# The order of the products inside an MLP layer's first matrix product: eight mixed orders, or three sweeps

## The chip, the cores and the metric

The kernel runs on one core of one Trainium2 chip. The metric is the time of one execution on the device in microseconds (us), taken as the median of several runs. Five engines work side by side, each on its own queue of instructions: TensorE (PE; its weight loads are shown as PEld), VectorE (DVE), ScalarE (ACT), GpSimd (POOL) and SyncE (SP), which here issues the transfers. PSUM is where matmuls add up their sums, SBUF where everything else lies.

## The reference

Two layers of a decoder trunk over 256 tokens of width 2048, each followed by an MLP of width 8192. All weights and all data are float32.

```python
def _mlp(h, w1, w2):
    u = jnp.einsum('bsd,df->bsf', h, w1)
    u = jnp.square(jax.nn.relu(u))
    return jnp.einsum('bsf,fd->bsd', u, w2)
...
    for i in range(DEPTH):
        h = _rmsnorm(x, mix_norm[i])
        j = i // N_MIXERS
        if i % N_MIXERS == 0:
            x = x + _rglru_block(h, ...)
        else:
            x = x + _dilated_attention_block(h, ...)
        x = x + _mlp(_rmsnorm(x, mlp_norm[i]), mlp_w1[i], mlp_w2[i])
    return _rmsnorm(x, final_norm)
```

## The kernel before

**Products in three parts.** Each float32 number is cut into a high part (its rounding to the type that TensorE multiplies, fp32r) and a low part (the rest, rounded too). A product is the sum of three: high weights by high data, high weights by low data, low weights by high data. The low by low product is left out.

**Units.** All weights come as units of 128 x 2048 numbers (1 MB) in the order in which they are used. For each unit SP issues a load into a `raw` buffer (3 of them, line 76), ScalarE copies it to the high tile `whi` (4 buffers, line 86), and VectorE subtracts to get the low tile `wlo` (3 buffers, line 90). `before_unit` (line 103) issues these ahead of the unit's products: loads 5 units ahead, high parts 3, low parts 2. The items of the program run in a fixed order; `after(n, ...)` puts a piece of follow-up work behind the item n places later. Every engine takes its instructions in the order in which they are issued.

**The data.** `xT` holds the layer's input, transposed: for each of 16 steps k (128 of the 2048 input features) a row of 512 columns, columns 0 to 255 the high part of the 256 tokens, columns 256 to 511 their low part. The four tiles `xT0` to `xT3` hold four steps each; `transpose_chunk` (lines 169 to 183) makes them, with TensorE transposes (line 176), ScalarE for the high part (line 158) and VectorE for the low part (line 159).

**The first MLP product** (`plan_mlp`, from line 504). The 8192 hidden features are worked on in four stretches of 16 units; a unit gives 128 hidden features for all 256 tokens. Its weights stand still in TensorE (128 x 128 a matmul), and the rows of `xT` move through. For each of the 16 steps there are the pieces ("h", k, 0, 256), ("h", k, 256, 512) and ("l", k, 0, 256): which weight tile, which step, which columns of `xT`; "h" with 0 to 512 is the first two in one matmul of 512 columns. `orders` (line 225) lists the pieces of a unit in one of seven styles, and each of the eight stretches (four in either MLP) has a style of its own. In the order of time: thirds, wide_first, pairs, apart in the first MLP, thirds_low_first, fours, thirds, as_was in the second. `stand_w2` (line 252) issues them through `mm` (line 141, one weight load and one matmul each) into a PSUM bank `acc` (four of them). In the two styles that begin with "thirds", all three pieces go into the same 256 columns of the bank; in the others the product with the tokens' low part has columns 256 to 511 for itself. In the first stretch of either MLP the first two units are done on steps 0 to 11 first, then on 12 to 15, since the last tile of `xT` is still being made.

**What follows a unit.** `u_done` (line 488): where there are two half sums, VectorE adds them (a reduction, line 493) and then takes the maximum with 0 and multiplies by the norm's factor (line 494); where there is one, a single instruction does the latter out of PSUM (line 491). ScalarE squares (line 496) and makes the high part `aT` (line 498); VectorE makes its low part one item later (line 502).

**The second MLP product** follows each stretch (`out_item`, line 281, and `stand_x`, line 265). There `aT` stands still and the weights move, 512 columns a matmul: high by high, high by low, low by high. It takes 16 units too. The recurrent layer's first projection uses `stand_w` (line 216) with the order high, high, low of "thirds".

Of the kernel before, what the change touches and what calls it, by code (L numbers as in the profile page):

```python
# [13 lines left out]
OP = mybir.AluOpType  # L14
AX = mybir.AxisListType

D = 2048
S = 256
# [31 lines left out]
def trunk(ctx: ExitStack, tc: tile.TileContext, a: dict, out: bass.AP):  # L50
    nc = tc.nc
# [10 lines left out]
    def unit(ap, width=UW):  # L62
        units.append((ap, width))
        return len(units) - 1
# [51 lines left out]
    def item(u, fn):  # L116
        items.append((u, fn))
# [20 lines left out]
    def after(n, fn, *args):  # L138
        later.setdefault(now[0] + n, []).append((fn, args))

    def mm(o, l, r, start, stop):
        nc.tensor.matmul(o, l, r, start=start, stop=stop, skip_group_check=True)  # L142
# [12 lines left out]
    state = {}  # L155
# [10 lines left out]
    def xT(k):  # L166
        return state["xT", k // 4][:, k % 4, :]
# [17 lines left out]
    def square_sum(n, ts=range(NT)):  # L185
        sq = state["ssq"]
        for t in ts:
            junk = perm.tile([P, 512], mybir.dt.bfloat16, name="junk")
            nc.scalar.activation(junk, xc[n][:, t, :], AF.Square, accum_out=sq[:, t, n:n + 1])  # L189

    def new_ssq():
        state["ssq"] = perm.tile([P, NT, NCH], F32, name="ssq", bufs=2)
# [29 lines left out]
            mm(ps, hi[:, s], x[:, 256:512], False, False)  # L222
            mm(ps, lo[:, s], x[:, 0:256], False, last and j == len(ks) - 1)

    def orders(style, ks):

        ks = list(ks)
        if style == "thirds":
            return [p for k in ks for p in (("h", k, 0, 256), ("h", k, 256, 512), ("l", k, 0, 256))]
        if style == "thirds_low_first":  # L230
            return [p for k in ks for p in (("l", k, 0, 256), ("h", k, 0, 256), ("h", k, 256, 512))]
        if style == "wide_first":
            return [p for k in ks for p in (("h", k, 0, 512), ("l", k, 0, 256))]
        if style == "pairs":
            return [p for a, b in zip(ks[::2], ks[1::2])
                    for p in (("l", a, 0, 256), ("l", b, 0, 256), ("h", b, 0, 512), ("h", a, 0, 512))]
        if style == "apart":
            return [("h", k, 0, 512) for k in ks] + [("l", k, 0, 256) for k in ks]
        if style == "fours":
            out = []  # L240
            for at in range(0, len(ks), 4):
                out += [("h", k, 0, 512) for k in ks[at:at + 4]] + [("l", k, 0, 256) for k in ks[at:at + 4]]
            return out
        out = []
        for k in ks:
            out += [("l", k, 0, 256), ("h", k, 0, 512)]
        return out

    def one_sum(style):
        return style.startswith("thirds")  # L250

    def stand_w2(ps, u, ks, w_at, first, last, style):
        hi, lo = split[u]
        todo = orders(style, ks)
        if first and todo[0][0] == "l" and not one_sum(style):

            at = next(i for i, p in enumerate(todo) if p[0] == "h")
            todo = [todo[at]] + todo[:at] + todo[at + 1:]
        for n, (w, k, c0, c1) in enumerate(todo):
            j = k - ks[0] + w_at  # L260
            s = slice(j * 128, (j + 1) * 128)
            o = ps[:, 0:256] if one_sum(style) else ps[:, c0:c1]
            mm(o, (hi if w == "h" else lo)[:, s], xT(k)[:, c0:c1], first and n == 0, last and n == len(todo) - 1)

    def stand_x(acc, u, get, ks, first, last, ts=range(NT)):
        hi, lo = split[u]
# [9 lines left out]
    def acc_tile():  # L276
        return psum.tile([P, 512], F32, name="acc", bufs=4)

    accs = {}
# [10 lines left out]
    def add_x(n, acc):  # L290
        for t in range(NT):
            nc.vector.tensor_add(xc[n][:, t, :], xc[n][:, t, :], acc[t])  # L292

    def close_chunk(n, gname, rows):
        def done(acc):
            if n == 0:
                new_ssq()
            add_x(n, acc)
            if n < NCH - 1:
                square_sum(n)  # L300
            after(1, transpose_chunk, n, gname)
            if n == NCH - 1:
                after(1, square_sum, n)
                after(1, rstd_cols)
                if rows:
                    after(4, rstd_rows)
        return done
# [4 lines left out]
    def new_aT(j):  # L312
        t = (perm if j < 16 else lru).tile([P, 512], F32R, name=f"aT{j}")
        state["aT", j] = t
        return t
# [169 lines left out]
                oproj(n, kq)  # L485


    def u_done(j, ps, style):
        r = lru.tile([P, S], F32, name="mr", bufs=2)
        if one_sum(style):  # L490
            nc.vector.scalar_tensor_tensor(r, ps[:, 0:256], 0.0, state["rstdB"], op0=OP.max, op1=OP.mult)  # L491
        else:
            nc.vector.tensor_reduce(r, ps.rearrange("p (b c) -> p c b", b=2), axis=AX.X, op=OP.add)  # L493
            nc.vector.scalar_tensor_tensor(r, r, 0.0, state["rstdB"], op0=OP.max, op1=OP.mult)  # L494
        uu = lru.tile([P, S], F32, name="mu", bufs=2)
        nc.scalar.activation(uu, r, AF.Square)  # L496
        t = new_aT(j)
        nc.scalar.activation(t[:, 0:256], uu, AF.Copy)  # L498
        after(1, u_low, t, uu)
# [1 line left out]
    def u_low(t, uu):  # L501
        nc.vector.tensor_sub(t[:, 256:512], uu, t[:, 0:256].bitcast(F32))  # L502

    def plan_mlp(w1, w2, done, styles):
        for c in range(4):
            us = []

            def part(j, ks, first, last, us=us, c=c, style=styles[c]):
                def run():
                    if first:  # L510
                        accs["u", j] = acc_tile()
                    stand_w2(accs["u", j], us[j], ks, ks[0], first, last, style)
                    if last:
                        after(1 if c == 0 and j == 0 else 0, u_done, j, accs.pop(("u", j)), style)
                item(us[j], run)

            us.extend(unit(w1[c * 16 + j]) for j in range(16))
            at = 0
            if c == 0:
                for j in range(2):  # L520
                    part(j, range(0, 12), True, False)
                for j in range(2):
                    part(j, range(12, 16), False, True)
                at = 2
            for j in range(at, 16):
                part(j, range(16), True, True)
            for n in range(NCH):
                last_c = c == 3
                if last_c and n == NCH - 1 and done is final_done:
                    final_items([unit(w2[(c * 4 + n) * 4 + kq]) for kq in range(4)])  # L530
                    continue
                for kq in range(4):
                    u = unit(w2[(c * 4 + n) * 4 + kq])
                    out_item(("m", n), u, aT, range(4 * kq, 4 * kq + 4), kq == 0, kq == 3,
                             done(n) if last_c else (lambda acc, n=n: add_x(n, acc)))
# [135 lines left out]
    def final_items(us):  # L671
        acc = {}

        def part(kq, ts):
            def run():
                if kq == 0:
                    for t in ts:
                        acc[t] = acc_tile()
                stand_x(acc, us[kq], aT, range(4 * kq, 4 * kq + 4), kq == 0, kq == 3, ts)
                if kq == 3:  # L680
                    for t in ts:
                        after(0, final_rows, acc[t], t)
            item(us[kq], run)

        part(0, range(NT))
        for t in range(NT):
            for kq in (1, 2, 3):
                part(kq, (t,))

    def load_g():  # L690
# [6 lines left out]
    first = [None] * 4  # L697
    lru.open("rec")
    plan_rec()
    item(None, lru.close)  # L700
    item(None, lambda: lru.open("mlp"))
    plan_mlp(a["w1_0"], a["w2_0"], lambda n: close_chunk(n, "mix1", False),
             ("thirds", "wide_first", "pairs", "apart"))
    item(None, lru.close)
    item(None, lambda: lru.open("att"))
    plan_att()
    item(None, lru.close)
    item(None, load_g)
    plan_mlp(a["w1_1"], a["w2_1"], final_done, ("thirds_low_first", "fours", "thirds", "as_was"))


    nc.sync.dma_start(par, a["par"])
# [16 lines left out]
    for n in range(NCH):  # L729
        xg[n] = perm.tile([P, 4, S], F32, name="xg", bufs=2)  # L730
        rs = [wts.tile([P, UW], F32, name="raw", bufs=RAW_BUFS) for _ in range(3)] if n == 0 else rs
        for h in range(2 if n == 0 else 1):
            w = 2 if n == 0 else 4
            nc.sync.dma_start(xg[n][:, h * w:(h + 1) * w, :], a["xT"][:, 4 * n + h * w:4 * n + (h + 1) * w, :])
            for i in range(3):
                if n or i == 0:
                    s = slice(n * 512 + h * w * 128, n * 512 + (h + 1) * w * 128)
                elif h:
                    s = slice(0, 512)
# [5 lines left out]
        for h in range(2 if n == 0 else 1):  # L745
            w = 2 if n == 0 else 4
# [5 lines left out]
            for i in range(3):  # L752
# [3 lines left out]
                for at, (s, _) in enumerate(raw[i]):  # L756
                    if s.stop == n * 512 + (h + 1) * w * 128:
# [5 lines left out]
                        ks = range(s.start // 128, s.stop // 128)  # L763
# [14 lines left out]
    for n in range(NCH):  # L778
        s = slice(n * 512, (n + 1) * 512)
        r = xc[n // 2][:, n % 2, :]  # L780
# [14 lines left out]
    ps = psum.tile([P, 2, S], F32, name="tr", bufs=2)  # L795
# [102 lines left out]
```

## Time and profile before

| | |
|---|---|
| median of 3 runs | 2198.01 us (2196.51 to 2198.35) |
| the profiled execution | 2199.65 us |
| its span, first to last instruction | 2197.9 us |
| TensorE busy | 2175.3 us (99%) |
| VectorE / ScalarE / GpSimd busy | 1280.0 us (58%) / 1061.3 us (48%) / 78.3 us (4%) |
| DMA | 188 GB/s in the mean |
| mean granted clock of TensorE | 0.996 |

The profile shows one execution. An engine's share is its busy time over the span. Matmuls overlap, and the end of each is modelled, so the distance between the starts of two of them says what one costs, and the duration column (276 to 398 ns) does not. Weight loads (PEld) run beside the matmul before. The chain that ended last goes back from the last instruction to what released it, step by step.

### The profile page before, as it was taken

How to read it: one execution, taken by the hardware profiler on the slowest of the kernel's cores; microseconds unless marked ns; L12 is line 12 of the kernel's file. 1: busy time of each engine (PE TensorE's matmuls, PEld its weight loads, DVE VectorE, ACT ScalarE, POOL GpSimd, SP SyncE). 2: the span in 40 equal slices, each digit the busy share in tenths (PEclk: the TensorE clock that was granted, in tenths of full speed). 3: DMA queues.
4: the chain of work that ended last, by engine and by line, in shares of the span. 5: the costliest groups of instructions: out<-in, count | busy, mean ns of one | idle time of the engine just before them, and what ended most of it. 6: DMA issues, size and time to landing. Idle time of an engine off the chain costs nothing.

```text
span 2197.9 us, 29494 instructions
## 1 busy us (share of the span) xinstructions
PE 2175.3 (99%) x12490; PEld 1910.4 (87%) x12490; DVE 1280.0 (58%) x1344; ACT 1061.3 (48%) x1163; POOL 78.3 (4%) x42
## 2 busy tenths in 40 slices
PE   7999999999999999999999999999999999999998
PEld 7999988998888888888888888889988889988886
DVE  8898855554564565565555555555546645545654
ACT  5787754543443343344445544555434434433442
POOL 2221100000000000000000000000000000000001
PEclk9999999999999999999999999999999999999999
DMA  6565555455555555555554445455555555555553
GB/s 219 211 211 194 194 207 189 175 192 191 191 183 201 185 188 197 189 189 194 181 192 166 159 174 183 161 188 199 200 195 181 198 196 184 186 193 189 191 192 115
DMA packets 61700, 413.40 MB, mean 188 GB/s; under 512 B 6784, under 2 KB 7168, under 8 KB 13440
## 3 DMA queue, kind: packets, MB, share of 16 engines
q1 hardware_dynamic: 61568, 411.51, 53.3%
q8 instruction: 98, 1.61, 0.3%
q14 instruction: 34, 0.28, 0.0%
HBM read 409.39 MB, written 2.10 MB: 187 GB/s over the span
## 4 chain that ended last, share of the span: by engine, by line
PE 96%; DVE 2%; ACT 1%; POOL 0%; DMA 0%; issue 0%; SPq 0%; DVEq 0%; ACTq 0%
PE acc L142 93%; PE g L142 1%; DVE wlo L90 1%; PE tr L176 0%; PE tr L568 0%; PE g L576 0%; DMA xg<-in_xT 0%; DVE xT L750 0%; PE tr L599 0%; POOL a L357 0%; ACT whi L86 0%; POOL c L358 0%; PE g L609 0%; PE g L608 0%; PE g L607 0%
## 5 line engine op out<-in xcount | busy, mean ns | idle before, releaser
L90 DVE TENSOR_TENSOR wlo<-raw,whi 128x2048 fp32r<-128x2048 f32 (+3 forms) x400 | 883.4, 2212 | 345.6 <-PE acc L142 267.9
L86 ACT ACTIVATE whi<-raw 128x2048 fp32r<-128x2048 f32 (+3 forms) x400 | 736.8, 1844 | 525.2 <-PE acc L142 437.6
L142 PE MATMUL acc<-xT,whi 128*128 128x256 f32 (+1 forms) x4064 | 882.7, 317 | 7.0 <-ACT whi L86 6.3
L142 PE MATMUL acc<-whi,aT 128*128 128x512 f32 x2624 | 813.9, 390 | 0.0
L142 PEld LDWEIGHTS acc<-xT,whi 128*128 128x128 f32 x4064 | 653.8, 190 | 46.4 <-ACT whi L86 6.7
L142 PE MATMUL acc<-xT,wlo 128*128 128x256 f32 x2672 | 654.9, 280 | 7.1 <-DVE wlo L90 6.8
L142 PEld LDWEIGHTS acc<-whi,aT 128*128 128x128 f32 x2624 | 492.6, 188 | 102.2
L142 PE MATMUL acc<-wlo,aT 128*128 128x512 f32 x1312 | 510.7, 389 | 0.0
L142 PEld LDWEIGHTS acc<-xT,wlo 128*128 128x128 f32 x2672 | 481.8, 190 | 27.6 <-DVE wlo L90 8.3
L142 PEld LDWEIGHTS acc<-wlo,aT 128*128 128x128 f32 x1312 | 246.3, 188 | 50.5
L142 PE MATMUL acc<-whi,xT 128*128 128x512 f32 x768 | 245.9, 395 | 0.0
L496 ACT ACTIVATE mu<-mr 128x256 f32<-128x256 f32 x128 | 53.5, 418 | 370.2 <-DVE mr L494 242.7
L142 PEld LDWEIGHTS acc<-whi,xT 128*128 128x128 f32 x768 | 144.3, 188 | 30.7
L142 PE MATMUL acc<-wlo,xT 128*128 128x512 f32 x384 | 150.4, 392 | 0.0
L493 DVE TENSOR_REDUCE mr<-acc 128x256 f32<-128x512 f32 x80 | 55.3, 692 | 156.1 <-PE acc L142 156.1
L292 DVE TENSOR_TENSOR xc<-xc,acc 128x512 f32<-128x512 f32 x78 | 53.2, 687 | 97.7 <-PE acc L142 97.7
L491 DVE SCALAR_TENSOR_TENSOR mr<-acc,rstdB 128x256 f32<-128x256 f32 x48 | 20.2, 424 | 112.9 <-PE acc L142 112.9
L142 PEld LDWEIGHTS acc<-wlo,xT 128*128 128x128 f32 x384 | 72.2, 188 | 15.1
L643 POOL TENSOR_TENSOR xc<-xc,gB 128x1024 f32<-128x1024 f32 x3 | 10.6, 3534 | 1879.9 <-DMA raw<-in_w 1843.4
L498 ACT ACTIVATE aT<-mu 128x256 fp32r<-128x256 f32 x128 | 53.6, 419 | 4.1
L502 DVE TENSOR_TENSOR aT<-mu,aT 128x256 fp32r<-128x256 f32 x128 | 53.4, 418 | 0.0
L189 ACT ACTIVATE junk<-xc 128x512 bf16<-128x512 f32 x32 | 20.2, 633 | 57.1 <-DVE xc L292 38.6
(143 smaller groups left out, 792.2 us busy)
## 6 DMA issues: line engine op xcount, KB each, us to landing
raw<-in_w SPq DMA_DIRECT2D x256, 1024.0 KB, 4.8
raw<-in_w_qkv SPq DMA_DIRECT2D x48, 1024.0 KB, 4.8
raw<-in_w_in SPq DMA_DIRECT2D x35, 1024.0 KB, 4.8
raw<-in_w_out SPq DMA_DIRECT2D x20, 1024.0 KB, 4.8
raw<-in_w_o SPq DMA_DIRECT2D x16, 1024.0 KB, 4.8
raw<-in_w_g SPq DMA_DIRECT2D x10, 512.0 KB, 3.3
raw<-in_w_in SPq DMA_DIRECT2D x11, 256.0 KB, 5.0
xc<-in_x SPq DMA_DIRECT2D x4, 512.0 KB, 5.7
```

Of the source, the lines that this page charges most:

```text
L86: nc.scalar.activation(split[i][0][:, s], r, AF.Copy)
L90: nc.vector.tensor_sub(split[i][1][:, s], r, split[i][0][:, s].bitcast(F32))
L142: nc.tensor.matmul(o, l, r, start=start, stop=stop, skip_group_check=True)
L189: nc.scalar.activation(junk, xc[n][:, t, :], AF.Square, accum_out=sq[:, t, n:n + 1])
L292: nc.vector.tensor_add(xc[n][:, t, :], xc[n][:, t, :], acc[t])
L491: nc.vector.scalar_tensor_tensor(r, ps[:, 0:256], 0.0, state["rstdB"], op0=OP.max, op1=OP.mult)
L493: nc.vector.tensor_reduce(r, ps.rearrange("p (b c) -> p c b", b=2), axis=AX.X, op=OP.add)
L496: nc.scalar.activation(uu, r, AF.Square)
L498: nc.scalar.activation(t[:, 0:256], uu, AF.Copy)
L502: nc.vector.tensor_sub(t[:, 256:512], uu, t[:, 0:256].bitcast(F32))
L643: nc.gpsimd.tensor_mul(xc[n], xc[n], state["gB"][:, None, n * 512:(n + 1) * 512].to_broadcast([P, NT, 512]))
```

## The change

All eight stretches of the first MLP product get the same order. A unit's 48 pieces go in three sweeps over its steps: low weights on the tokens' high part for all steps, then high weights on the high part for all steps, then high weights on the low part for all steps. Every matmul has 256 columns, and all three sweeps add into the same 256 columns of the bank. The first piece of the first sweep clears the sum, the last piece of the third ends it. In the two units that are done in two parts, each part has its own three sweeps. The styles, the reduction over two half sums and `one_sum` go. Cut to its core:

```diff
-    def orders(style, ks):
+    def sweeps(ks):
 
         ks = list(ks)
-        if style == "thirds":
-            return [p for k in ks for p in (("h", k, 0, 256), ("h", k, 256, 512), ("l", k, 0, 256))]
...
-    def stand_w2(ps, u, ks, w_at, first, last, style):
+        return ([("l", k, 0, 256) for k in ks] + [("h", k, 0, 256) for k in ks]
+                + [("h", k, 256, 512) for k in ks])
+
+    def stand_w2(ps, u, ks, w_at, first, last):
         hi, lo = split[u]
-        todo = orders(style, ks)
-        if first and todo[0][0] == "l" and not one_sum(style):
-
-            at = next(i for i, p in enumerate(todo) if p[0] == "h")
-            todo = [todo[at]] + todo[:at] + todo[at + 1:]
+        todo = sweeps(ks)
         for n, (w, k, c0, c1) in enumerate(todo):
-            j = k - ks[0] + w_at
-            s = slice(j * 128, (j + 1) * 128)
-            o = ps[:, 0:256] if one_sum(style) else ps[:, c0:c1]
-            mm(o, (hi if w == "h" else lo)[:, s], xT(k)[:, c0:c1], first and n == 0, last and n == len(todo) - 1)
+            s = slice((k - ks[0] + w_at) * 128, (k - ks[0] + w_at + 1) * 128)
+            mm(ps, (hi if w == "h" else lo)[:, s], xT(k)[:, c0:c1], first and n == 0, last and n == len(todo) - 1)
...
-    def u_done(j, ps, style):
+    def u_done(j, ps):
         r = lru.tile([P, S], F32, name="mr", bufs=2)
-        if one_sum(style):
-            nc.vector.scalar_tensor_tensor(r, ps[:, 0:256], 0.0, state["rstdB"], op0=OP.max, op1=OP.mult)
-        else:
-            nc.vector.tensor_reduce(r, ps.rearrange("p (b c) -> p c b", b=2), axis=AX.X, op=OP.add)
-            nc.vector.scalar_tensor_tensor(r, r, 0.0, state["rstdB"], op0=OP.max, op1=OP.mult)
+        nc.vector.scalar_tensor_tensor(r, ps[:, :S], 0.0, state["rstdB"], op0=OP.max, op1=OP.mult)
...
-                    stand_w2(accs["u", j], us[j], ks, ks[0], first, last, style)
+                    stand_w2(accs["u", j][:, :S], us[j], ks, ks[0], first, last)
...
-    plan_mlp(a["w1_0"], a["w2_0"], lambda n: close_chunk(n, "mix1", False),
-             ("thirds", "wide_first", "pairs", "apart"))
+    plan_mlp(a["w1_0"], a["w2_0"], lambda n: close_chunk(n, "mix1", False))
...
-    plan_mlp(a["w1_1"], a["w2_1"], final_done, ("thirds_low_first", "fours", "thirds", "as_was"))
+    plan_mlp(a["w1_1"], a["w2_1"], final_done)
```

## Rows read from the trace of the kernel before

**Rows 1.** The page: span, TensorE's busy time, its granted clock, the chain by engine.

```profile
span 2197.9 us, 29494 instructions
...
PE 2175.3 (99%) x12490; PEld 1910.4 (87%) x12490; DVE 1280.0 (58%) x1344; ACT 1061.3 (48%) x1163; POOL 78.3 (4%) x42
...
PEclk9999999999999999999999999999999999999999
...
PE 96%; DVE 2%; ACT 1%; POOL 0%; DMA 0%; issue 0%; SPq 0%; DVEq 0%; ACTq 0%
```

**Rows 2.** Lines 491 and 493, each stretch: ns min/median/max, first and last start.

```profile
L491 DVE SCALAR_TENSOR_TENSOR mr<-acc,rstdB x14: 423/424/425, 402.3 to 475.7; 128x256 f32<-128x256 f32 x14
...
L493 DVE TENSOR_REDUCE mr<-acc x16: 690/692/692, 568.4 to 653.2; 128x256 f32<-128x512 f32 x16
...
L493 DVE TENSOR_REDUCE mr<-acc x16: 690/691/692, 745.9 to 829.3; 128x256 f32<-128x512 f32 x16
...
L493 DVE TENSOR_REDUCE mr<-acc x16: 691/692/693, 921.9 to 1005.1; 128x256 f32<-128x512 f32 x16
...
L491 DVE SCALAR_TENSOR_TENSOR mr<-acc,rstdB x14: 423/426/427, 1501.1 to 1571.8; 128x256 f32<-128x256 f32 x14
...
L493 DVE TENSOR_REDUCE mr<-acc x16: 691/692/693, 1664.4 to 1747.6; 128x256 f32<-128x512 f32 x16
...
L491 DVE SCALAR_TENSOR_TENSOR mr<-acc,rstdB x16: 423/424/425, 1840.3 to 1925.1; 128x256 f32<-128x256 f32 x16
...
L493 DVE TENSOR_REDUCE mr<-acc x16: 690/692/692, 2017.8 to 2102.4; 128x256 f32<-128x512 f32 x16
```

**Rows 3.** Timeline of TensorE in "apart": start us, length us, what, count.

```profile
927.24 3.89 PE L142 MATMUL acc<-xT,whi 128*128 128x512 f32 x16
930.97 1.98 PE L142 MATMUL acc<-xT,wlo 128*128 128x256 f32 x16
932.79 3.89 PE L142 MATMUL acc<-xT,whi 128*128 128x512 f32 x16
936.51 1.98 PE L142 MATMUL acc<-xT,wlo 128*128 128x256 f32 x16
```

**Rows 4.** Timeline of TensorE in the second MLP product.

```profile
499.80 0.61 PE L142 MATMUL acc<-whi,aT 128*128 128x512 f32 x2
500.26 0.39 PE L142 MATMUL acc<-wlo,aT 128*128 128x512 f32 x1
500.48 0.61 PE L142 MATMUL acc<-whi,aT 128*128 128x512 f32 x2
```

**Rows 5.** Groups by form (mean ns) at 106-127, 403-475, 1484-1487 and 1501-1571 us.

```profile
L142 PE MATMUL acc<-xT,whi 128*128 128x256 f32 x128 | 21.8, 276 | 0.0
...
L142 PE MATMUL acc<-xT,whi 128*128 128x256 f32 x410 | 72.5, 281 | 0.0
...
L142 PE MATMUL acc<-xT,whi 128*128 128x256 f32 x17 | 3.1, 281 | 0.0
...
L142 PE MATMUL acc<-xT,whi 128*128 128x256 f32 x413 | 70.3, 276 | 0.0
```

**Rows 6.** Windows: us, PE, PEld, DVE, ACT, POOL busy (count), PEclk, DMA, GB/s.

```profile
916.40:1004.60 88.20, 88.20 (x510) 76.71 (x509) 57.65 (x62) 41.49 (x46) 0.00 (x0) 1.00 0.53 184
1501.00:1571.40 70.40, 70.40 (x624) 70.40 (x623) 38.47 (x39) 34.45 (x39) 0.00 (x0) 1.00 0.56 199
```

**Rows 7.** The page's groups: busy us, mean ns, idle before it, releaser.

```profile
L90 DVE TENSOR_TENSOR wlo<-raw,whi 128x2048 fp32r<-128x2048 f32 (+3 forms) x400 | 883.4, 2212 | 345.6 <-PE acc L142 267.9
...
L493 DVE TENSOR_REDUCE mr<-acc 128x256 f32<-128x512 f32 x80 | 55.3, 692 | 156.1 <-PE acc L142 156.1
```

**Rows 8.** Timeline of VectorE before the first MLP product: the last xT tiles.

```profile
364.09 1.29 DVE L159 TENSOR_TENSOR xT<-xg,xT 128x512 fp32r<-128x512 f32 x2 [5.12 <-ACT xT L158]
...
391.00 1.29 DVE L159 TENSOR_TENSOR xT<-xg,xT 128x512 fp32r<-128x512 f32 x2 [3.77 <-ACT xT L158]
```

**Rows 9.** The page's DMA issues: KB each, median us to landing.

```profile
raw<-in_w SPq DMA_DIRECT2D x256, 1024.0 KB, 4.8
```

More of the change, by code (lines that the diff above doesn't have):

```diff
@@ L223, in stand_w @@
             mm(ps, lo[:, s], x[:, 0:256], False, last and j == len(ks) - 1)
-    def orders(style, ks):
+    def sweeps(ks):
         ks = list(ks)
-        if style == "thirds":
-            return [p for k in ks for p in (("h", k, 0, 256), ("h", k, 256, 512), ("l", k, 0, 256))]
[L230 to L250, printed above, removed]
-    def stand_w2(ps, u, ks, w_at, first, last, style):
+        return ([("l", k, 0, 256) for k in ks] + [("h", k, 0, 256) for k in ks]
+                + [("h", k, 256, 512) for k in ks])
+    def stand_w2(ps, u, ks, w_at, first, last):
         hi, lo = split[u]
-        todo = orders(style, ks)
-        if first and todo[0][0] == "l" and not one_sum(style):
-            at = next(i for i, p in enumerate(todo) if p[0] == "h")
-            todo = [todo[at]] + todo[:at] + todo[at + 1:]
+        todo = sweeps(ks)
         for n, (w, k, c0, c1) in enumerate(todo):
-            j = k - ks[0] + w_at
-            s = slice(j * 128, (j + 1) * 128)
-            o = ps[:, 0:256] if one_sum(style) else ps[:, c0:c1]
-            mm(o, (hi if w == "h" else lo)[:, s], xT(k)[:, c0:c1], first and n == 0, last and n == len(todo) - 1)
+            s = slice((k - ks[0] + w_at) * 128, (k - ks[0] + w_at + 1) * 128)
+            mm(ps, (hi if w == "h" else lo)[:, s], xT(k)[:, c0:c1], first and n == 0, last and n == len(todo) - 1)
     def stand_x(acc, u, get, ks, first, last, ts=range(NT)):
@@ L502, in u_low, with plan_mlp, part @@
         nc.vector.tensor_sub(t[:, 256:512], uu, t[:, 0:256].bitcast(F32))
-    def plan_mlp(w1, w2, done, styles):
+    def plan_mlp(w1, w2, done):
         for c in range(4):
             us = []
-            def part(j, ks, first, last, us=us, c=c, style=styles[c]):
+            def part(j, ks, first, last, us=us, c=c):
                 def run():
@@ L511, in run @@
                         accs["u", j] = acc_tile()
-                    stand_w2(accs["u", j], us[j], ks, ks[0], first, last, style)
+                    stand_w2(accs["u", j][:, :S], us[j], ks, ks[0], first, last)
                     if last:
-                        after(1 if c == 0 and j == 0 else 0, u_done, j, accs.pop(("u", j)), style)
+                        after(1 if c == 0 and j == 0 else 0, u_done, j, accs.pop(("u", j)))
                 item(us[j], run)
```

## The prediction

> **What bounds the kernel now.** I read the head of the page first: TensorE is busy for 99% of the span, its granted clock stands at 9 tenths or more in every slice, and the chain that ended last is 96% TensorE [rows 1]. So a change is worth what it saves or adds between one matmul's start and the next, and hardly anything else.
>
> The next view is the one line behind each of the 128 units of the first MLP product that reads its finished sum; the distance between its first and last instruction, divided by the count less one, is the time of a unit [rows 2]. The arithmetic is the same everywhere: a step costs 768 columns, a unit 12,288. The eight stretches differ only in their order, and their units take, in the order of time: 73.4/13 = 5.646 us, 84.8/15 = 5.653, 83.4/15 = 5.560, 83.2/15 = 5.547, 70.7/13 = 5.438, 83.2/15 = 5.547, 84.8/15 = 5.653 and 84.6/15 = 5.640. The sum is 44.684 us, so 16 units of each are 714.9 us of the span. The reader is to see two things. First, orders with equal work differ by up to 4%, and TensorE idles in none of them: it is busy for the whole of each window, at granted clock 1.00, that is 2.4 GHz [rows 6]. Second, "thirds" has three weight loads a step and "wide_first" two, at the same 5.65 us, so that a third load as such costs nothing.
>
> The timeline tells more. In the second MLP product, three matmuls of 512 columns take 0.68 us, 0.227 each [rows 4]. Half of that is 0.113 us for 256 columns, and the unit of 5.438 us is 48 of these. I call this the fast pace (113.3 ns per 256 columns) and that of the 5.653 us unit the slow one (117.8 ns). In the duration column, the profile's model of a single matmul, they show as 276 and 281 ns [rows 5].
>
> The same rows hold a warning: the order alone doesn't fix the pace. High, high, low runs at 276 in the recurrent projection and at 281 in the first stretch of the MLP; low, high, high runs at 281 before the last transposes of its stretch and at 276 behind them [rows 5]. Both orders go on at the pace at which they once are.
>
> **The change, part by part.** The one stretch that already has whole sweeps is "apart" [rows 3]. Its sweep of 16 low pieces, 256 columns each, takes 930.97 to 932.79 = 1.82 us, 113.8 ns a piece: the fast pace with about 0.01 us lost at its start. Its sweep of 16 high pieces of 512 takes 927.24 to 930.97 = 3.73 us, 233 ns a piece, against the 227 of [rows 4].
>
> *The low sweep* (16 pieces of 256, new in six stretches and moved to the front in two) is this row itself: 1.82 us.
>
> *The two high sweeps* are not in the trace. Their nearest rows are two. The low sweep has the same width, the same step through the weight tile and the same step through xT, and differs in the tile that it reads: 1.82 us for each. The wide high sweep has the same weights, at twice the width. If its loss of 3.73 − 16 x 0.227 = 0.10 us goes with columns, a narrow high sweep is 1.865 us; if it goes with instructions, each of the 16 keeps 6.4 ns of it and the sweep is 16 x 0.1197 = 1.915 us. I take 1.82: 256-column pieces read high weights at the fast pace in two rows of [rows 5], so the tile as such isn't the cause, and the low sweep is the nearer row in width and in step. From below, a sweep of 48/3 pieces of the 5.438 us unit is 1.813 us, and no row shows less.
>
> *The sum.* A unit becomes 3 x 1.82 = 5.46 us, 128 of them 698.9 us: 714.9 − 698.9 = 16.0 us less. Of this the two "thirds" stretches, "wide_first" and "as_was" give 0.18 to 0.19 us a unit, "pairs", "apart" and "fours" 0.09 to 0.10, and "thirds_low_first" loses 0.02. At the lower bound (1.813) the gain is 18.6 us.
>
> *More instructions.* In five stretches a step has three matmuls and three loads where it had two, 80 x 16 = 1,280 more of each. By the rows, two pieces of 256 at the fast pace take what one of 512 does, so I add nothing; the bounds above hold the case that each costs 6.4 ns. The Trainium skill, "TensorE: Matmul & The Clock Gate", section "Back-to-back issue gap", gives an isolated matmul its columns and a fixed 2.5 ns; by that rule, as an estimate, the 1,280 would take 3.2 us back and the gain would be 12.8 us. The trace disagrees at these widths: 5.438 us / 48 is half of 0.227 us, with nothing left for a fixed part.
>
> *The epilogue.* The 80 reductions over the two half sums, 0.69 us each [rows 7], go, 55 us of VectorE. VectorE is busy for 57.65 of 88.20 us in "apart" [rows 6], and TensorE goes on into another bank meanwhile, so this is worth 0. Without that cover it would be 0.69 us at the end of each of the 80 units. What follows the sum (mu, aT) comes 0.7 us sooner, and no one waits for it.
>
> *Low weights first.* A unit now needs its whole wlo at its first matmul. The subtraction (2.21 us, [rows 7]) is issued two units ahead, some 7 us before it is needed at 5.46 us a unit. "thirds_low_first" already needs it at once, at a faster unit, and TensorE is busy for all of its 70.40 us [rows 6]: 0. wlo's slot is free after the first sweep, but the next subtraction stands behind the epilogue on VectorE's queue, which waits for the whole sum; so it starts no earlier. The high weights are needed 1.8 us later than now, and held as long.
>
> *The first two units of each MLP*, on steps 0 to 11 and then 12 to 15, read the high half of xT at 12 steps in 1.4 us instead of 4. Steps 8 to 11 were made at 364 us, long before the product starts at about 384, and steps 12 to 15 at 391.0 to 392.3, with the four last steps due at about 393.4 [rows 8]: 0.
>
> *Loads.* A unit takes one load of 1 MB, 4.8 us from issue to landing [rows 9], and "thirds_low_first" runs at one in 5.44 us: 0. SP's and POOL's queues keep their order.
>
> The sum is made against the profiled execution: span 2197.9 us, execution 2199.65 us, which is 1.6 us over the median 2198.01 us. The span loses 16.0 us, and so does the median: **2182.0 us**.
>
> **The rivals.**
>
> *The high sweeps lose per instruction.* Each piece of the two high sweeps keeps the 6.4 ns that the wide high sweep loses, or the whole unit starts slow behind the second product and stays so; both come to 1.82 + 2 x 1.915 = 5.65 us and 48 x 117.8 ns = 5.65 us. Then 128 units take 723.6 us, 8.7 more: 2206.7 us, slower. It decides where a high piece takes over 117.7 ns ((44.684/8 − 1.82) / 32). For it: in "apart" the high sweep falls off the fast pace although the low sweep before it held it, and two orders of 256-column pieces stay slow for whole stretches [rows 5]. Against it: the low sweep comes back to the fast pace within itself, out of a slow high sweep [rows 3]; what a stretch of one kind of piece does here, the orders that mix kinds don't.
>
> *The high sweeps lose per column.* 1.82 + 2 x 1.865 = 5.55 us, what "apart" and "fours" have now: 710.4 us, 4.5 less, 2193.5 us. For it: the same rows, if the loss comes from reading xT in long runs of high weights. Against it: two sweeps of 256 each skip half of every step's columns, as the low sweep does.
>
> *The change does nothing to the pace*, each stretch staying as it starts: some sweeps fast, some slow, between these two, about 2190 to 2200 us.
>
> **How the numbers follow.** About 0.2% of the time (4.4 us) can be told from no change. I give my forecast 0.60, the loss per instruction or lasting slow pace 0.20, the loss per column 0.16, the mixture 0.04. The loss per column lies just at 0.2%, so 0.09 of it counts as faster and 0.07 as no change; the mixture gives 0.01 to faster, 0.02 to no change and 0.01 to slower. Faster is 0.60 + 0.09 + 0.01 = 0.70, the same 0.09, slower 0.21. The range begins a little under the lower bound of 1.813 us a sweep (2198.0 − 18.6 = 2179.4) and ends above the loss per column and the mixture, at 2200; what it leaves out is the slow rival, 0.20. The forecast's own range is 2179 to 2187.
>
> **What would show it.** Right: in all eight stretches the line that reads the sum comes every 5.44 to 5.47 us; the 256-column matmuls have a mean duration of 276 or 277 ns with high weights as with low; each sweep of the timeline takes 1.81 to 1.83 us; TensorE waits for no wlo. The per-instruction rival shows as low sweeps of 1.82 and high ones of 1.9, the lasting slow pace as three of 1.88 with 281 ns throughout, the per-column one as high sweeps of 1.865. I am wrong if the two high sweeps aren't like the low one, or if a new wait appears ahead of the first sweep.

## The result, and the profile after

The changed kernel takes **2204.74 us** (median of 7 runs, 2204.01 to 2205.57), the kernel before 2198.44 us in the 7 runs beside it. The ratio is 1.0029, with a 95% interval of 1.0019 to 1.0039: slower by 0.3%. The forecast was 2182.0 us, and the time lies outside its range of 2178 to 2200. The profiled execution took 2204.83 us, its span is 2203.1 us, 5.2 more than before.

The first lines of the page, to hold against [rows 1]:

```profile
span 2203.1 us, 32009 instructions
...
PE 2180.4 (99%) x13770; PEld 1972.9 (90%) x13770; DVE 1224.4 (56%) x1264; ACT 1061.8 (48%) x1163; POOL 77.1 (4%) x42
```

The counts are those of the change: 13,770 − 12,490 = 1,280 matmuls more, 80 VectorE instructions fewer. TensorE waits no more than before, 13.6 us in all against 13.8:

```profile
PE acc L142 <- DVE wlo L90: 6.8, 4, 2.7
PE acc L142 <- ACT whi L86: 5.7, 1, 5.7
PE acc L142 <- DVE xT L718: 1.1, 2, 0.9
```

These are the waits of TensorE over the whole span (us in total, times, longest). All of them lie ahead of the first MLP, which starts at 384 us. In the windows of the next block, in stretch 2 and in stretch 5, TensorE is busy for the whole time, at granted clock 1.00 in both, and so are the weight loads. The columns are those of [rows 6]:

```profile
562.43:652.89 90.46, 90.46 (x770) 90.45 (x768) 47.47 (x48) 41.64 (x46) 0.00 (x0) 1.00 0.53 185
1510.00:1570.00 60.00, 60.00 (x531) 60.00 (x531) 32.71 (x34) 29.31 (x34) 0.00 (x0) 1.00 0.54 195
```

The line that reads a unit's sum answers to [rows 2], one row for each stretch (first and last start, without the two units that are done in parts):

```profile
L463 DVE SCALAR_TENSOR_TENSOR mr<-acc,rstdB x14: 424/425/425, 402.1 to 475.6; 128x256 f32<-128x256 f32 x14
...
L463 DVE SCALAR_TENSOR_TENSOR mr<-acc,rstdB x16: 424/425/425, 568.3 to 653.1; 128x256 f32<-128x256 f32 x16
L463 DVE SCALAR_TENSOR_TENSOR mr<-acc,rstdB x16: 424/425/425, 745.8 to 830.6; 128x256 f32<-128x256 f32 x16
L463 DVE SCALAR_TENSOR_TENSOR mr<-acc,rstdB x16: 424/425/425, 923.3 to 1008.1; 128x256 f32<-128x256 f32 x16
...
L463 DVE SCALAR_TENSOR_TENSOR mr<-acc,rstdB x14: 423/426/427, 1504.0 to 1574.7; 128x256 f32<-128x256 f32 x14
...
L463 DVE SCALAR_TENSOR_TENSOR mr<-acc,rstdB x16: 424/425/425, 1667.5 to 1752.3; 128x256 f32<-128x256 f32 x16
L463 DVE SCALAR_TENSOR_TENSOR mr<-acc,rstdB x16: 424/425/425, 1844.9 to 1929.7; 128x256 f32<-128x256 f32 x16
L463 DVE SCALAR_TENSOR_TENSOR mr<-acc,rstdB x16: 424/425/425, 2022.4 to 2107.2; 128x256 f32<-128x256 f32 x16
```

Seven stretches run at 84.8/15 = 5.653 us a unit (73.5/13 = 5.654 in the first), which is the slow pace to the third digit: 48 x 117.8 ns. The fifth runs at 70.7/13 = 5.438 us, the fast pace, at the same granted clock. No stretch is in between any more. The account closes by stretch: "pairs" loses 0.093 us a unit, "apart" and "fours" 0.106 each, "as_was" 0.013, the two "thirds", "wide_first" and "thirds_low_first" nothing. That is 0.318 x 16 = 5.1 us of the 5.2 that the span gained. **The whole loss is that the four stretches which ran between the two paces ("pairs", "apart", "fours", "as_was") now run at the slow one.**

The timeline of the changed kernel shows the same sweeps at both paces (start us, length us, what, count). First the two units in parts at the head of stretch 1, then a unit of stretch 2, then the head of stretch 5 and a later unit of it:

```profile
383.99 1.53 PE L142 MATMUL acc<-xT,wlo 128*128 128x256 f32 x12
385.36 2.89 PE L142 MATMUL acc<-xT,whi 128*128 128x256 f32 x24
388.08 1.04 PE L176 MATMUL tr<-con,xc 128*128 128x128 f32 x8
388.88 1.66 PE L142 MATMUL acc<-xT,wlo 128*128 128x256 f32 x12
390.37 2.99 PE L142 MATMUL acc<-xT,whi 128*128 128x256 f32 x24
393.20 0.64 PE L142 MATMUL acc<-xT,wlo 128*128 128x256 f32 x4
...
573.74 2.05 PE L142 MATMUL acc<-xT,wlo 128*128 128x256 f32 x16
575.62 3.93 PE L142 MATMUL acc<-xT,whi 128*128 128x256 f32 x32
579.39 0.28 PE L142 MATMUL acc<-xT,wlo 128*128 128x256 f32 x1
...
1487.38 2.99 PE L142 MATMUL acc<-xT,whi 128*128 128x256 f32 x24
1490.21 1.03 PE L176 MATMUL tr<-con,xc 128*128 128x128 f32 x8
...
1498.15 0.38 PE L209 MATMUL tr<-con,rs 128*128 128x128 f32 x2
1498.28 2.08 PE L142 MATMUL acc<-xT,wlo 128*128 128x256 f32 x16
1500.20 3.79 PE L142 MATMUL acc<-xT,whi 128*128 128x256 f32 x32
1503.82 1.41 PE L142 MATMUL acc<-xT,wlo 128*128 128x256 f32 x11
...
1509.26 1.98 PE L142 MATMUL acc<-xT,wlo 128*128 128x256 f32 x16
1511.08 1.64 PE L142 MATMUL acc<-xT,whi 128*128 128x256 f32 x13
```

The reader is to compare starts. The first unit's 24 high pieces take 388.08 − 385.36 = 2.72 us, 113 ns each; then eight transposes pass, and the second unit's 24 take 393.20 − 390.37 = 2.83 us, 118 ns each, in the same order and on the same xT. In stretch 2 the low sweep takes 1.88 us and the two high ones 3.77, so low and high pieces are slow alike; in stretch 5 the low sweep takes 1.82. Stretch 5 begins slow too: the 24 high pieces of its first unit take 1490.21 − 1487.38 = 2.83 us. Its second unit, in parts like the first, is as slow, and then two transposes of 128 columns (line 209) come, and behind them the 32 high pieces of the third unit take 1503.82 − 1500.20 = 3.62 us. In stretch 1 the same two transposes stand at the same place and leave the stretch slow. The rival in which the high sweeps lose per instruction is wrong in its mechanism, for high pieces are as fast as low ones where the low ones are fast. What is left is its other half, a pace that lasts, and that changes in places where small matmuls come in between.

### The profile page after: what moved, and what is told of

Its sections match the earlier page's. It is cut to its first block, busy times and chain, and to the rows that moved or that the text cites. A ratio compares the mean times of both kernels' runs of the same rounds, so it can differ in the third digit from the quotient of the medians.

```text
span 2203.1 us, 32009 instructions
## 1 busy us (share of the span) xinstructions
PE 2180.4 (99%) x13770; PEld 1972.9 (90%) x13770; DVE 1224.4 (56%) x1264; ACT 1061.8 (48%) x1163; POOL 77.1 (4%) x42
## 4 chain that ended last, share of the span: by engine, by line
PE 96%; DVE 1%; ACT 1%; DMA 1%; POOL 0%; issue 0%; SPq 0%; DVEq 0%; ACTq 0%
PE acc L142 93%; PE g L142 1%; DMA raw<-in_w_in 1%; PE tr L176 0%; DVE wlo L90 0%; PE tr L537 0%; PE g L545 0%; PE tr L568 0%; POOL a L330 0%; DVE xT L718 0%; ACT whi L86 0%; POOL c L331 0%; PE g L578 0%; PE g L577 0%; PE g L576 0%
## 5 line engine op out<-in xcount | busy, mean ns | idle before, releaser
L142 PE MATMUL acc<-xT,whi 128*128 128x256 f32 x5344 | 723.8, 281 | 6.8 <-ACT whi L86 5.7
L142 PEld LDWEIGHTS acc<-xT,whi 128*128 128x128 f32 x5344 | 684.5, 190 | 7.6 <-ACT whi L86 6.1
L142 PE MATMUL acc<-xT,wlo 128*128 128x256 f32 x2672 | 439.0, 281 | 7.0 <-DVE wlo L90 6.8
L142 PEld LDWEIGHTS acc<-xT,wlo 128*128 128x128 f32 x2672 | 370.7, 190 | 9.0 <-DVE wlo L90 8.3
L463 DVE SCALAR_TENSOR_TENSOR mr<-acc,rstdB 128x256 f32<-128x256 f32 x128 | 54.2, 425 | 329.3 <-PE acc L142 328.8
L159 DVE TENSOR_TENSOR xT<-xg,xT 128x512 fp32r<-128x512 f32 x24 | 15.5, 689 | 53.9 <-ACT xT L158 53.9
```

The costliest lines, as they stand in the source:

```text
L159: nc.vector.tensor_sub(lo_out, src, hi_out.bitcast(F32))
L463: nc.vector.scalar_tensor_tensor(r, ps[:, :S], 0.0, state["rstdB"], op0=OP.max, op1=OP.mult)
```

## The experiments

The theory after this reading (A): the pace is carried from one matmul to the next, and is set by what comes ahead of a stretch. Its rivals: sweeps as an order are slow (B); the pace belongs to the stretch, by what runs beside it or by its data (C). Later ones concern the place of the weights in memory: it sets the pace (D), it does so by getting a matmul's columns and the weight load in each other's way (E), or one place alone is special (F). A time without an interval is that of one run; there, differences of a few us are read from unit times, not from the total. The kernel before took 2196.1 to 2199.1 us (medians) beside these runs.

**Another order, no sweeps (e1).**

```diff
-        return ([("l", k, 0, 256) for k in ks] + [("h", k, 0, 256) for k in ks]
-                + [("h", k, 256, 512) for k in ks])
+        return [p for k in ks for p in (("l", k, 0, 256), ("h", k, 0, 256), ("h", k, 256, 512))]
```

> All eight stretches in the order low, high, high of one step after another, 256 columns each, no sweeps. Theory A (the pace is carried from matmul to matmul and set where a stretch begins; the order of 256-column pieces doesn't matter): the same stretches are slow and fast as with the sweeps, seven units of 5.65 us and one of 5.44, 2204 to 2206 us. Rival B (sweeps as such are slow, the order that mixes kinds is fast): all stretches at 5.44 us a unit, about 2182 us.

Measured: 2203.57 us. The rows of stretches 2 and 5:

```profile
L462 DVE SCALAR_TENSOR_TENSOR mr<-acc,rstdB x16: 424/425/425, 567.0 to 651.8; 128x256 f32<-128x256 f32 x16
...
L462 DVE SCALAR_TENSOR_TENSOR mr<-acc,rstdB x14: 423/426/427, 1502.7 to 1573.4; 128x256 f32<-128x256 f32 x14
```

They take 5.653 and 5.438 us a unit, and the other six are slow as well. So "thirds_low_first" was the fastest order of the kernel before by its position alone: it stood in stretch 5. B falls.

**A few units in wide pieces (e2).** The sweeps stay, but the units named in the expectation take 512-column pieces and two half sums (with the reduction for them).

```diff
+        if style == "apart":
+            return [("h", k, 0, 512) for k in ks] + [("l", k, 0, 256) for k in ks]
+        if style == "one":
+            return ([("h", 0, 0, 512)] + [("l", k, 0, 256) for k in ks] + [("h", k, 0, 256) for k in ks[1:]]
+                    + [("h", k, 256, 512) for k in ks[1:]])
...
-        todo = sweeps(ks)
+        todo = wides(style, ks) if style else sweeps(ks)
```

> Sweeps as in the change, but single units are done in 512-column pieces with two half sums: the first unit of the stretches 2, 3, 4 (wide_first, pairs, apart) and 6 (one wide piece, the rest 256), the first and the ninth of stretch 7 (apart), the ninth of stretch 8 (one wide piece). Theory A: the sweeps behind pairs and apart go on at 5.44 us a unit to the end of their stretch, that is 15 x 0.21 = 3.2 us less for each; behind wide_first and one wide piece open. Rival C (the pace belongs to the stretch: what runs beside it, or its data): a few matmuls behind the wide unit the pace is back at 5.65 us a unit.

Measured: 2189.21 us. Behind "pairs", "apart" and "one" every unit takes 5.44 us to the end of its stretch; behind "wide_first" 5.65. In stretch 8 the change of pace shows in the middle. Its timeline around the ninth unit, whose one wide piece lies in the second row's 33:

```profile
2042.33 2.05 PE L142 MATMUL acc<-xT,wlo 128*128 128x256 f32 x16
2044.21 4.16 PE L142 MATMUL acc<-xT,whi 128*128 128x256 f32 x33
2048.22 1.99 PE L142 MATMUL acc<-xT,wlo 128*128 128x256 f32 x16
2050.04 3.56 PE L142 MATMUL acc<-xT,whi 128*128 128x256 f32 x30
2053.44 1.98 PE L142 MATMUL acc<-xT,wlo 128*128 128x256 f32 x16
2055.25 0.96 PE L142 MATMUL acc<-xT,whi 128*128 128x256 f32 x7
```

The low sweep takes 1.88 us ahead of the wide piece and 1.82 and 1.81 behind it. C falls: same stretch, same tiles, same work beside, and the pace is another one for good after a single matmul. This also fits what "pairs", "apart" and "fours" did in the kernel before: there the pace moved within every unit, and they ran at a mean of it. In "pairs" the starts in the trace lie 227, 235, 118 and 113 ns apart (two wide pieces, two low ones), over and over; in "wide_first", which stayed slow, 235 and 118.

**One additional matmul at the head (e3) or in the middle (e4).**

```diff
+    def nudge(u, width, count):
+        tr = psum.tile([P, 2, S], F32, name="tr", bufs=2)
+        for _ in range(count):
+            mm(tr.rearrange("p a c -> p (a c)")[:, 0:width], split[u][0][:, 0:128], xT(0)[:, 0:width], True, True)
...
+                        for width, count in nudges.get((c, j), ()):
+                            nudge(us[j], width, count)
```

> Sweeps as in the change, with one additional matmul ahead of the first unit of six stretches, into a bank that nobody reads: 32, 64, 128, 256, 512 columns, and two of 128. Theory A: some of the widths put their stretch on the fast pace, 5.44 us a unit for all its 16 units (3.4 us less each), others leave it; 256 and 512 should leave it, as these are what comes anyway. Rival C: no width changes anything beyond its own 0.03 to 0.3 us.

> Sweeps as in the change, with one additional matmul ahead of a unit in the middle: 128, 64, 32 columns ahead of the ninth unit of stretches 2, 3, 4; 128 ahead of the ninth unit of stretch 5, which is at the fast pace; twice in stretches 6, 7, 8 (128, 192, 96 columns, ahead of the fifth and the eleventh unit). Theory A: where a width puts the pace to fast in a slow stretch, the units before it take 5.65 us and those behind it 5.44; a width may also put the fast stretch to slow. Rival C: unit times change nowhere.

Measured: 2195.9 and 2201.43 us. The unit times behind each additional matmul:

| columns | where | pace ahead | pace behind |
|---|---|---|---|
| 32 | head of stretch 2; ninth unit of stretch 4 | slow | slow |
| 64 | head of stretch 3; ninth unit of stretch 3 | slow | fast |
| 96 | fifth, eleventh unit of stretch 8 | slow, fast | fast, slow |
| 128 | head of stretch 4; ninth of 2; fifth of 6 | slow | slow |
| 128 | eleventh unit of stretch 6; ninth of 5 | slow; fast | fast; slow |
| 2 x 128 | head of stretch 8 | slow | fast |
| 192 | fifth, eleventh unit of stretch 7 | slow, fast | fast, fast |
| 256 / 512 | head of stretch 6 / 7 | slow | slow / fast |

The part of the expectation on 512 columns was wrong: they put the pace to fast. The two turns in the middle are plain in e4's timeline, 64 columns in stretch 3 and 128 in stretch 5:

```profile
779.91 2.05 PE L142 MATMUL acc<-xT,wlo 128*128 128x256 f32 x16
781.80 3.93 PE L142 MATMUL acc<-xT,whi 128*128 128x256 f32 x32
785.57 0.19 PE L142 MATMUL tr<-xT,whi 128*128 128x64 f32 x1
785.60 2.08 PE L142 MATMUL acc<-xT,wlo 128*128 128x256 f32 x16
787.52 3.79 PE L142 MATMUL acc<-xT,whi 128*128 128x256 f32 x32
791.15 1.07 PE L142 MATMUL acc<-xT,wlo 128*128 128x256 f32 x8
...
1526.39 3.79 PE L142 MATMUL acc<-xT,whi 128*128 128x256 f32 x32
1530.02 0.22 PE L142 MATMUL tr<-xT,whi 128*128 128x128 f32 x1
1530.08 2.10 PE L142 MATMUL acc<-xT,wlo 128*128 128x256 f32 x16
1532.01 3.93 PE L142 MATMUL acc<-xT,whi 128*128 128x256 f32 x32
1535.78 1.46 PE L142 MATMUL acc<-xT,wlo 128*128 128x256 f32 x11
```

In stretch 3 the 32 high pieces take 3.77 us ahead and 3.63 behind; in stretch 5 it is 3.63 ahead and 3.77 behind. A single matmul of 0.03 to 0.06 us turns the pace of all that follows, in either direction. The same 128 columns turn it in one place and not in another. In the four places where a single 128 met a stretch that was slow, it turned it once, at the eleventh unit of stretch 6, behind another 128 at the fifth; and two in a row turned it at the head of stretch 8. So in both cases it was the second 128 that turned it. That the slow pace has more than one state inside is the nearest explanation; no row shows these states, and each case is one run.

**The fast pace everywhere (e7), and in another order (e8).** Seven matmuls of 64 columns, at the head of stretches 2, 3, 4, 6, 7, 8 and ahead of the third unit of stretch 1; e8 has the order of e1 besides.

```diff
-    plan_mlp(a["w1_1"], a["w2_1"], final_done)
+    plan_mlp(a["w1_1"], a["w2_1"], final_done, {(1, 0): [(64, 1)], (2, 0): [(64, 1)], (3, 0): [(64, 1)]})
```

> The change with one additional matmul of 64 columns, into a bank that nobody reads, at the head of the six stretches that begin behind a second product, and ahead of the third unit of the first stretch. Theory A: all stretches run at 5.44 us a unit from there on. 6 x 16 x 0.213 + 14 x 0.213 = 23.4 us less than the change, some 0.1 us each spent at the start: 2204.7 - 22.8 = 2181.9 us, faster than the kernel before by 0.75%. Rival C (64 columns were chance in the two places tried): part of the stretches stays at 5.65 us, 2185 to 2203 us.

> The same seven additional matmuls, with the order low, high, high of one step after another in place of the sweeps. Theory A with the order of 256-column pieces without effect: 2181 to 2183 us, as with sweeps. Rival B' (the order decides how a stretch takes the additional matmul): some stretches stay slow, 2185 us or more.

Measured: e7 2179.67 us (5 runs, 2177.35 to 2182.01), ratio to the kernel before 0.9921, interval 0.9908 to 0.9935: **faster than both kernels**, by 0.8% than the one before. e8 took 2181.37 us. e7's rows of stretches 1 and 2:

```profile
L468 DVE SCALAR_TENSOR_TENSOR mr<-acc,rstdB x14: 424/426/427, 400.5 to 471.2; 128x256 f32<-128x256 f32 x14
...
L468 DVE SCALAR_TENSOR_TENSOR mr<-acc,rstdB x16: 424/426/427, 563.9 to 645.5; 128x256 f32<-128x256 f32 x16
```

That is 70.7/13 and 81.6/15, 5.44 us a unit, and so in all eight. The order of 256-column pieces is worth nothing that can be seen; the state in which they start is worth 23 us by the unit times (110 units, 0.213 us each). The median lies 25.1 us below the change's, but these are two groups of runs, and the kernel before differed by 2.3 us between them.

**The place of the weights (e5, e6, e9 to e12).** An unused tile behind xT moves everything that lies behind it, all weight tiles and aT among it, away from xT. In the program as built xT starts at a multiple of 256 bytes within a partition and the weight tiles 64 bytes behind one; all tiles of a kind are multiples of 256 apart. The traces hold no addresses. The sizes in the kernel agree with the distance: between xT and the weights lie tiles of 1024, 2 x 32, 2 x 1024 and 16 x 2048 bytes, together 64 over a multiple of 256.

```diff
+        if n == NCH - 1:
+            nc.vector.memset(perm.tile([P, 112], F32, name="pad"), 0.0)
```

112 columns are 448 bytes; the other runs have 64, 16, 32, 8 and 24.

> The change, with an unused tile of 448 bytes a partition behind xT, so that the weight tiles (and aT) lie 448 bytes further from xT than before; order and counts of the matmuls as in the change. Theory A (the pace is carried, set by what comes ahead): the same stretches slow and fast, 2203 to 2206 us. Rival D (the pace comes from where weights and xT lie towards each other): other stretches are slow, or none: between 2182 and 2206 us.

> The same with 256 bytes in place of 448. Theory A: 2203 to 2206 us, the same stretches slow and fast. Rival D: a pattern of its own, unlike both the change and the run with 448.

> The change with an unused tile of 64 bytes a partition behind xT, so that the weight tiles start 128 bytes behind a multiple of 256 where xT starts at one (0 in the run with 448, 64 in the change and in the run with 256). Theory E (a matmul's columns and the weight load beside it get in each other's way by their place modulo 256 bytes; at 64 there are two lasting paces, at 0 one, 120 ns): another set of paces than 113.3, 117.8 and 120 ns, or one of them throughout the stretches; if it is the fast one throughout, about 2182 us. Rival F (only 0 is special, all else has the two paces): 2203 to 2206 us.

> The same with 128 bytes: weight tiles 192 bytes behind a multiple of 256. Theory E: one pace or a set of its own, and by symmetry with 64 perhaps the two paces again. Rival F: 2203 to 2206 us, the two paces of the change.

> The change with an unused tile of 32 bytes a partition behind xT: weight tiles 96 bytes behind a multiple of 256, half way between 64 (two paces, 113.3 and 117.8 ns) and 128 (120 ns in the mean, no other). If what counts is a piece of 64 bytes that a place falls into: as with 64 or as with 128, 2204 or 2230 us. If places count by the byte: paces of its own, in between, or the fast one throughout (about 2182 us).

> The same with 96 bytes: weight tiles 160 bytes behind a multiple of 256, half way between 128 and 192. By pieces of 64 bytes: as with 128 or as with 192, 2230 or 2206 us; by the byte: a set of its own, the mirror of the run with 32.

Measured, with the unit time from a line once a unit (ScalarE's copy into aT, first to last start over 15, in stretch 2; in stretch 5 from the third unit on, over 13):

| run | bytes added | weights modulo 256 | time us | unit in stretch 2, us | unit in stretch 5, us |
|---|---|---|---|---|---|
| the change | 0 | 64 | 2204.74 | 5.65 | 5.44 |
| e6 | 256 | 64 | 2200.33 | 84.8/15 = 5.65 | 5.44 |
| e11 | 32 | 96 | 2221.95 | 85.4/15 = 5.69 | 5.63 |
| e9 | 64 | 128 | 2230.59 | 86.4/15 = 5.76 | 5.70 |
| e12 | 96 | 160 | 2232.10 | 86.4/15 = 5.76 | 5.76 |
| e10 | 128 | 192 | 2205.99 | 84.8/15 = 5.65 | 5.44 |
| e5 | 448 | 0 | 2224.83 | 86.4/15 = 5.76 | 5.76 |

The rows behind it, for 448, 256, 64, 128, 32 and 96 bytes:

```profile
L467 ACT ACTIVATE aT<-mu x16: 417/418/418, 576.0 to 662.4; 128x256 fp32r<-128x256 f32 x16
```

```profile
L467 ACT ACTIVATE aT<-mu x16: 418/418/420, 564.6 to 649.4; 128x256 fp32r<-128x256 f32 x16
```

```profile
L467 ACT ACTIVATE aT<-mu x16: 418/418/421, 577.1 to 663.5; 128x256 fp32r<-128x256 f32 x16
```

```profile
L467 ACT ACTIVATE aT<-mu x16: 418/420/422, 565.4 to 650.2; 128x256 fp32r<-128x256 f32 x16
```

```profile
L467 ACT ACTIVATE aT<-mu x16: 417/419/421, 574.5 to 659.9; 128x256 fp32r<-128x256 f32 x16
```

```profile
L467 ACT ACTIVATE aT<-mu x16: 417/418/421, 575.6 to 662.0; 128x256 fp32r<-128x256 f32 x16
```

Where the weights lie, modulo 256 bytes, decides which paces there are. At 64 and 192 they are 113.3 and 117.8 ns; at 0 and 160 all stretches run at 5.76 us / 48 = 120.0 ns; at 128 it is 120.0 and, in the first stretch of either MLP, 118.7, at 96 118.7 and, in the first stretch of either MLP, 117.3. These are means over a unit. In stretch 2 the starts lie 120 ns apart one like the other at 0, but 117, 120 and 123 in turn at 128, and between 115 and 125 in longer rounds at 96 and 160. So 120.0 at 128 and 160 is not the pace that 0 has.

Rival F falls (128, 96 and 160 are special too), and so does a piece of 64 bytes as the unit, since 96 is like neither 64 nor 128; it isn't the mirror of 160 either. Theory A alone expected e5 at the time of the change: it is incomplete. Rival D expected a gain or no change from e5, and a pattern of its own for e6, and had neither. (e6 has the change's paces in every stretch; 4.5 us of its lower time lie ahead of the MLP, whose second unit ends that much sooner.) Theory E's paces of its own came at 128, and the two paces again at 192; its mechanism isn't shown by that. The pace is carried, but among those that the placement leaves open. No place gave the fast pace to all stretches, though 192 gave it to the first as well, at 70.8/13 = 5.45 us a unit:

```profile
L467 ACT ACTIVATE aT<-mu x14: 417/418/420, 401.9 to 472.7; 128x256 fp32r<-128x256 f32 x14
```

xT was never moved itself, so a place of the weights towards xT and a place as such are not told apart by these runs. In the second product, where weights and aT are moved alike, 512 columns take 226.7 to 226.9 ns in the mean in every one of them; that speaks for the place of the two towards each other, and doesn't prove it.

## Why the prediction was wrong

**The step that failed** is the cost of the high sweeps and, under it, that of the low one: "The low sweep ... is this row itself: 1.82 us". The row was right for "apart", where 16 wide pieces of the same product come just ahead of it, and the sweep is at the fast pace from its second piece on. In the new order no such piece comes ahead (at the head of a stretch the second product's 512 columns do, and leave it slow), and the sweep takes 1.88 us, like everything else in its stretch. The prediction had the facts for this: it wrote that both orders of [rows 5] "go on at the pace at which they once are". It then set them aside with the sentence that a stretch of one kind of piece comes back to the fast pace within itself. "apart" doesn't show that: it shows a sweep behind a wide piece, and e2 shows that a wide piece alone can put all that follows to the fast pace. "thirds_low_first", too, mixes the kinds and was the fastest of all.

**The rival on the slow side** named the right outcome, "the whole unit starts slow behind the second product and stays so", with 2206.7 us, 8.7 more. The span grew by 5.2 us. The difference is stretch 5, which the rival took to be slow: 16 x 0.213 = 3.4 us. Its other mechanism, a loss of each high piece, and the rival of a loss per column are both wrong: high pieces are as fast as low ones (2.72 us for 24).

**What held.** The third load and the 1,280 additional matmuls cost nothing: "wide_first" had 512 matmuls in its stretch and now has 768, at 5.653 us a unit both times, and e7's 768 a stretch run at half of 0.227 us each. The Trainium skill, "TensorE: Matmul & The Clock Gate", section "Back-to-back issue gap", gives an isolated matmul a fixed 2.5 ns besides its columns; in the streams measured here no such fixed part shows between 256 and 512 columns. The 80 reductions were worth 0 behind TensorE, as costed, TensorE waits for no low weights in either MLP, and the loads of 1 MB kept up with 5.44 us a unit in e7, where it waits for nothing there either. The fast pace for all three sweeps exists as predicted: e7's unit is 5.44 us against 5.46. Only what puts a stretch on it wasn't in the change.

**Open.** What the pace is physically. That its choice depends on the placement modulo 256 bytes may mean that the weight load and the moving columns, or another engine's access to the same tiles, get in each other's way; no run here shows that they do. The Trainium skill, "SBUF — State Buffer", section "Who interferes with whom", gives TensorE two read ports that are independent of each other. Whether the runs go against that is open, since no port was measured; but moving the weights by 64 bytes takes the matmul from 113.3 or 117.8 ns to 118.7 or 120.0, and for the time it takes that measurement decides, whatever the mechanism. Open too are the states inside the slow pace, and why the two transposes of line 209 turn stretch 5 and not stretch 1.

## What to carry to other kernels

Before a row is used as the price of an instruction, look whether the same instruction in the same order has another price elsewhere in the trace; if it has, the order isn't the cause, and what stands ahead of it must be copied too. Where several variants run in one kernel, each in one place, their ranking can be that of the places. And in a TensorE-bound kernel compare the start-to-start time with the lowest one of that width anywhere in the trace: here a matmul of 64 columns in the right place was worth more than every order.

## What the runs showed of the hardware that was not expected

- Back-to-back matmuls of 256 columns in fp32r have two lasting paces at granted clock 1.00, with the tiles placed as in the change: 113.3 and 117.8 ns from start to start, kept over the 768 matmuls of a stretch. A single matmul of 64 columns turned slow to fast in each of the eight places where it was put; a single one of 128 did so in one of four, where another had gone before, and turned fast to slow in the fifth.
- 512 columns behind one another in the second product take 0.227 us in both kernels and in all runs, whatever the pace of the 256-column stretch ahead; in the change the first product starts slow behind them in the six stretches that follow a second product of their own MLP.
- Weights 0, 96, 128 or 160 bytes off a multiple of 256, with xT on one, gave no unit at 113.3 ns a matmul in the first product; the best mean was 117.3, and the kernel took 17 to 27 us more than the change, in one run each.
